# The prompt's down projection in seven Strassen products of halves, its second residual prepared during the up projection

## The chip, the cores and the metric

The kernel runs on one core of a Trainium2 chip. The time of a run is the device time in microseconds, from start to end of the program on that core. A core has a matrix engine (TensorE, PE in the profile; its weight loads are PEld), VectorE (DVE), ScalarE (ACT), GpSimd (POOL) and SyncE (SP), which issues most transfers. Each has its own queue of instructions, worked off in order; they wait for each other through semaphores.

## The reference

One layer for a prompt of 1024 tokens and a sample of 32, all in float32. The change touches only what follows the attention: the convolutional feed-forward block, and the second residual and norm.

```python
def _post_norm(x, h, gate, g, b):
    y = DEEPNORM_ALPHA * x.astype(jnp.float32) + gate.astype(jnp.float32) * h.astype(jnp.float32)
    mu = jnp.mean(y, axis=-1, keepdims=True)
    var = jnp.mean(jnp.square(y - mu), axis=-1, keepdims=True)
    return ((y - mu) * lax.rsqrt(var + LN_EPS) * g + b).astype(x.dtype)

def _conv_ffn(u, conv_prev, w_up, conv_w, conv_b, w_down):
    ...
    h = jax.nn.silu(conv) * b
    return jnp.einsum('btf,fd->btd', h, w_down), a_pad[:, -(CONV_WIDTH - 1):]

    # in _layer
    x = _post_norm(x, h, g1, ln1_g, ln1_b)
    u2 = x * (1.0 + sc2) + sh2
    f_out, conv_state = _conv_ffn(u2, conv_prev, w_up, conv_w, conv_b, w_down)
    x = _post_norm(x, f_out, g2, ln2_g, ln2_b)
```

The width of the model is 1024, that of the feed-forward block 2816, so `w_down` is 2816x1024 and the prompt's h is 1024x2816.

## The kernel before

Every large product is formed from float32 operands that are split in two (`split`, L85: ScalarE casts the value to a rounded high part, VectorE subtracts it to get the low part), and three products of the parts are summed in PSUM (`mm3`, L89). A product works on 128 rows of the contraction, 128 tokens as weights of the array and up to 512 output columns.

The stages around the change, in program order:

- The output projection (L855 and on) leaves each token block's normed result, without gain and bias, in the DRAM tile `dx1`, and its modulated transpose as `u2h` and `u2l` in SBUF.
- The up projection (L1071 to L1111) runs 22 passes `j` of 128 feed-forward columns, with two halves `s` (gate branch and the other). The weights of a half come through `up_weights` (L987) and `weights` (L860): a load on SP's queue into `raw`, the split into `wh` and `wl`, two buffers of each in the pool `pw`. After half 0 ScalarE copies the result into `row`, GpSimd sets the two columns ahead of it and keeps the convolution's state (L1087 to L1094), VectorE forms the convolution (L1095 to L1097), ScalarE applies SiLU (L1098). After half 1 VectorE multiplies into `hT[j]` (L1103 to L1105), 128 columns of h by 1056 tokens, which stays in SBUF.
- The down projection (L1115 to L1204) is `token_products` (L871): the eight blocks of 128 prompt tokens and the block of 32 sample tokens run in three groups, `groups = [[0, 1, 2, 8], [3, 4, 5], [6, 7]]`, each over 22 steps `k` of the contraction. In a step, `prepare` (L880) loads and splits a 128x1024 slice of the weights and splits a 128x384 (or 256) slice of h; it runs two steps ahead of the products, and its buffers alternate between the pools `pw` and `pf`, so that there are four of each. A step has 6 products for each prompt block (two halves of 512 columns) and 4 for the sample. In the last group the products of the last 4 steps are held and done block by block (L940).
- After a group `evacuate2` (L1143) multiplies the accumulators by the gate `g2p` out of PSUM (VectorE, L961 or L965), and later, spread over the next group's steps, adds the residual (L1148), forms the moments (L971, L975, L977 on VectorE, a power on GpSimd, L978) and scales (L1157, L1158), then stores. For the last two blocks `finish` (L1161) does this right away in small pieces.
- The second residual is ALPHA·(`dx1`·ln1_g + ln1_b). `residual` (L1134) loads a block of `dx1` and forms it on GpSimd during the down projection, 8 operations of 256 columns for a block; `begin2` (L1123) calls it late in each group.

The order of the instructions on each engine is made by the framework's scheduler from the program's order and its own estimate of times, except where `manual_schedule` stands. A tile's buffer is free for the next tile of its tag when all readers of the old one are done; a pool that is opened where another was closed waits for the old tiles at the same place.

## Time and profile before

| | us |
|---|---|
| median of 3 runs | 1597.68 |
| lowest, highest run | 1596.52, 1601.83 |
| the profiled execution, its own time | 1596.38 |
| its span in the trace | 1594.1 |

The trace is of one execution, and every number below is of that one; between its own time and its span lie 2.3 us. In a row, PE's busy time counts matmuls that overlap in the array, so a busy PE isn't yet PE at its best pace. Two records of one engine that follow each other overlap a little. A wait or a gap is put down to what ended it.

### The profile page before, as it was taken

How to read it: one execution, taken by the hardware profiler on the slowest of the kernel's cores; microseconds unless marked ns; L12 is line 12 of the kernel's file. 1: busy time of each engine (PE TensorE's matmuls, PEld its weight loads, DVE VectorE, ACT ScalarE, POOL GpSimd, SP SyncE). 2: the span in 40 equal slices, each digit the busy share in tenths (PEclk: the TensorE clock that was granted, in tenths of full speed). 3: DMA queues.
4: the chain of work that ended last, by engine and by line, in shares of the span. 5: the costliest groups of instructions: out<-in, count | busy, mean ns of one | idle time of the engine just before them, and what ended most of it. 6: DMA issues, size and time to landing. Idle time of an engine off the chain costs nothing.

```text
span 1594.1 us, 22475 instructions
## 1 busy us (share of the span) xinstructions
PE 1513.3 (95%) x8657; PEld 1266.8 (79%) x8657; DVE 798.5 (50%) x1552; ACT 569.0 (36%) x1123; POOL 365.5 (23%) x496
## 2 busy tenths in 40 slices
PE   6999999988999999899899999999999999997985
PEld 4677778755646777777799999999999988876874
DVE  4522325733536899557852333233323345377495
ACT  3211211244637788545532121112111233332342
POOL 0002014744413343134300000000000005054052
PEclk9999999998999999999999999999999999999998
DMA  9523312579764433445411111111111135344362
GB/s 270 164 95 111 94 46 107 147 194 240 196 185 119 126 77 96 125 162 207 140 54 41 53 40 53 41 53 40 54 41 54 40 129 205 106 149 135 132 207 83
DMA packets 166796, 183.83 MB, mean 115 GB/s; under 512 B 7458, under 2 KB 131907, under 8 KB 166691
## 3 DMA queue, kind: packets, MB, share of 16 engines
q1 hardware_dynamic: 158642, 155.84, 32.3%
q0 software_dynamic: 7760, 26.04, 5.6%
q8 instruction: 68, 1.11, 0.3%
q10 hardware_dynamic: 288, 0.52, 0.1%
q14 instruction: 38, 0.30, 0.1%
HBM read 151.94 MB, written 22.05 MB: 109 GB/s over the span
## 4 chain that ended last, share of the span: by engine, by line
PE 80%; DVE 7%; DMA 4%; issue 2%; POOL 2%; SPq 2%; ACT 2%; POOLq 0%; DVEq 0%; ACTq 0%
PE up L80 21%; PE upc L80 10%; PE wd L80 6%; PE wo L80 4%; PE po L80 3%; PE Sf L80 2%; PE ptf L114 2%; PE Sd L80 2%; PE pod L80 1%; POOL rs L1140 1%; SPq L171 1%; PE wd2y L80 1%; PE wd2x L80 1%; DMA wrfq<-in_w_in 1%; DMA adan<-in_w_ada 1%
## 5 line engine op out<-in xcount | busy, mean ns | idle before, releaser
L1093 POOL COPY cvo<-row 128x2 f32<-128x2 f32 x22 | 20.2, 918 | 385.4 <-ACT row L1091 385.4
L86 ACT CAST wdt<-h 128x384 fp32r<-128x384 f32 (+1 forms) x66 | 31.5, 478 | 160.4 <-PE wd5y L80 70.6
L1140 POOL TENSOR_TENSOR rs<-rs,ag 128x256 f32<-128x256 f32 x32 | 40.1, 1279 | 148.3 <-DMA rs<-dx 125.5
L625 POOL TENSOR_SCALAR wf<-wf,rs 128x128 f32<-128x128 f32 (+7 forms) x64 | 47.4, 745 | 109.2 <-DVE rs L591 71.9
L87 DVE TENSOR_TENSOR wdt<-h,wdt 128x384 fp32r<-128x384 f32 (+1 forms) x66 | 36.7, 556 | 67.8 <-ACT wdt L86 67.7
L1090 ACT COPY row<-up 128x352 f32<-128x352 f32 x44 | 17.8, 458 | 135.3 <-PE up L80 135.3
L1098 ACT ACTIVATE cv<-cv 128x1058 f32<-128x1058 f32 x22 | 24.0, 1089 | 95.5 <-DVE cv L1097 95.5
L590 ACT ACTIVATE wf<-wf,lo 128x128 f32<-128x128 f32 (+7 forms) x64 | 49.5, 776 | 18.3 <-DVE lo L587 16.0
L86 ACT CAST wh<-wr 128x512 fp32r<-128x512 f32 x40 | 24.3, 621 | 85.2 <-DMA wr<-in_w_in 19.3
L590 ACT ACTIVATE wd<-wd,lo 128x128 f32<-128x128 f32 (+7 forms) x64 | 49.6, 776 | 13.9 <-DVE lo L587 11.9
L80 PE MATMUL po<-ptpf,vf 128*64 128x256 f32 (+1 forms) x320 | 53.9, 374 | 0.5 <-DVE ptpf L615 0.4
L87 DVE TENSOR_TENSOR wh<-wr,wh 128x512 fp32r<-128x512 f32 x40 | 28.6, 738 | 51.1 <-ACT wh L86 51.1
L587 DVE CUSTOM_DVE_ANT_0 wf<-Sf,nb 128x512 f32<-128x512 f32 (+3 forms) x64 | 36.9, 589 | 28.5 <-PE Sf L80 21.3
L114 PE MATMUL ptf<-cst,wf 128*128 128x128 f32 x288 | 47.8, 287 | 1.1 <-POOL wf L625 0.7
L114 PEld LDWEIGHTS ptf<-cst,wf 128*128 128x128 f32 x288 | 32.2, 144 | 18.6 <-issue 9.3
L1103 DVE TENSOR_TENSOR h<-up,cv 128x352 f32<-128x352 f32 x44 | 21.0, 520 | 45.1 <-PE up L80 44.0
L80 PEld LDWEIGHTS po<-ptpf,vf 128*64 128x64 f32 x320 | 29.0, 138 | 18.0 <-issue 6.7
L650 POOL TENSOR_SCALAR wd<-wd,rs,lam 128x128 f32<-128x128 f32 (+7 forms) x32 | 26.5, 827 | 64.4 <-DVE rs L591 63.4
L1104 DVE TENSOR_TENSOR h<-upc,cv 128x320 f32<-128x320 f32 x22 | 10.8, 492 | 57.5 <-PE upc L80 57.5
L587 DVE CUSTOM_DVE_ANT_0 wd<-Sd,zero 128x512 f32<-128x512 f32 (+3 forms) x64 | 36.6, 583 | 1.7 <-PE Sd L80 1.3
L80 PE MATMUL pod<-ptpd,vd 128*128 128x256 f32 (+1 forms) x160 | 35.2, 362 | 0.4 <-ACT sq L667 0.3
L80 PEld LDWEIGHTS pod<-ptpd,vd 128*128 128x128 f32 x160 | 29.2, 191 | 4.4 <-ACT sq L667 0.9
(2698 smaller groups left out, 5032.9 us busy)
## 6 DMA issues: line engine op xcount, KB each, us to landing
wr<-in_w_in SPq DMA_DIRECT2D x20, 512.0 KB
adam<-in_w_ada SPq DMA_DIRECT2D x32, 256.0 KB
adan<-in_w_ada SPq DMA_DIRECT2D x32, 256.0 KB
ga<-in_w_ada SPq DMA_DIRECT2D x16, 512.0 KB
out<-z POOLq DMA_DIRECT2D x12, 512.0 KB, 4.0
x<-in_x_prompt SPq DMA_DIRECT2D x8, 512.0 KB
nb<-dcump SPq DMA_DIRECT2D x8, 512.0 KB
xp<-in_x_prompt SPq DMA_DIRECT2D x8, 512.0 KB
```

What stands on the lines that cost most here:

```text
L80: nc.tensor.matmul(out, l, r, start=start, stop=stop, **k)
L86: nc.scalar.copy(hi, src)
L87: (eng or nc.vector).tensor_tensor(lo, src, f(hi), ALU.subtract)
L114: nc.tensor.transpose(out, in_, ident[:n, :n])
L587: nc.vector.tensor_tensor_reduce(w[:, c], S[:, 0:n], t, -1.0, lo, ALU.add, ALU.min, lo_)
L590: nc.scalar.activation(w[:, 0:ext], w[:, 0:ext], AF.Exp, bias=lo, scale=-1.0, accum_out=sm)
L625: nc.gpsimd.tensor_scalar(w, w, rs, 1.0, ALU.mult, ALU.mult)
L650: nc.gpsimd.tensor_scalar(e1, e1, r1, lam, ALU.mult, ALU.mult)
L1093: nc.gpsimd.tensor_copy(cvo[:, 0, :, j], row[:, T:T + 2])
L1098: nc.scalar.activation(c[:, 0:L], c[:, 0:L], AF.Silu)
L1103: nc.vector.tensor_tensor(h[:, cs], accs[g], c[:, cs], ALU.mult)
L1140: nc.gpsimd.tensor_tensor(r[:, c], r[:, c], ag[0:n, c], ALU.mult)
```

## The change

The prompt's down projection is a product of 1024x2816 by 2816x1024. Both are cut into 2x2 halves (512 tokens; 1408 rows of the contraction, 11 steps of 128; 512 output columns), and the seven products of Strassen's scheme are formed in seven phases (`PHASES`), each with four blocks of 128 tokens by 512 columns over 11 steps, in four of six PSUM banks. Where a factor is a sum or difference, VectorE forms that of h and GpSimd that of the weights before the split. After a phase each accumulator is copied (ScalarE) or added (VectorE) into one or two quarters of the result, which is kept in SBUF as `ys`. The sample's 32 tokens are formed as before, over the weight halves that four of the phases have split anyway (`sam`). The gate is applied to the sums by GpSimd (`gate_and_add`), for blocks 0 to 3 in phase 5 and for blocks 4 to 7 in phase 6; `finish` adds the last product of blocks 4 to 7. The products of the last three steps of phase 6 are held and done block by block.

The second residual is formed during the up projection: `residuals` takes four steps in each of the first 18 passes, each a 128x128 piece of `dx1` loaded, multiplied and added on GpSimd, and stored to the new DRAM tile `dres`, from which the down projection loads blocks as they are.

The pool `pw` is closed before the down projection, and `px` is opened in its place. The operands' buffers are `xt` (two), `x2` (three, for the second slice of the weights) and `ot` (two in `px`, two in `pf`).

In the up projection:

```diff
+        def residuals():
+            for c0 in range(0, D, P):
+                c = slice(c0, c0 + P)
+                gb = pe.tile([P, 2, P], F32, name=f"gb{c0}", tag="gb", bufs=1)
+                for i, n in enumerate(("ln1_g", "ln1_b")):
+                    nc.sync.dma_start(gb[:, i], a[n][:, c].to_broadcast([P, P]))
+                nc.gpsimd.tensor_scalar(gb, gb, ALPHA, 0.0, ALU.mult, ALU.add)
+                for b in range(9):
+                    n = rows(b)
+                    r = pe.tile([P, P], F32, name=f"rr{c0}{b}", tag="rr", bufs=2)[0:n]
+                    nc.sync.dma_start(r, dx1[b * P:b * P + n, c])
+                    nc.gpsimd.tensor_tensor(r, r, gb[0:n, 0], ALU.mult)
+                    nc.gpsimd.tensor_tensor(r, r, gb[0:n, 1], ALU.add)
+                    nc.sync.dma_start(dres[b * P:b * P + n, c], r)
+                    yield
+        resid = residuals()
         for j in range(NJ):
+            for _ in range(4):
+                next(resid, None)
```

The down projection's `begin2`, `residual`, `evacuate2`, its `finish` and the call of `token_products` go, and in their place stands:

```diff
+    pwp.__exit__(None, None, None)
+    psum("psd", m=6, po=1, ms=1)
+    NK = NJ // 2
+    PHASES = [
+        (((0, 0), (1, 1), 1), ((0, 0), (1, 1), 1), ((0, 0, 1), (1, 1, 1)), None),
+        (((1, 1), None, 0), ((1, 0), (0, 0), -1), ((0, 0, 1), (1, 0, 1)), (0, "b")),
+        (((0, 0), (1, 0), 1), ((1, 1), None, 0), ((0, 0, -1), (0, 1, 1)), (1, "ab")),
+        (((0, 0), None, 0), ((0, 1), (1, 1), -1), ((0, 1, 1), (1, 1, 1)), (1, "a")),
+        (((1, 0), (1, 1), -1), ((1, 0), (1, 1), 1), ((0, 0, 1),), None),
+        (((0, 1), (1, 1), 1), ((0, 0), None, 0), ((1, 0, 1), (1, 1, -1)), (0, "ab")),
+        (((0, 1), (0, 0), -1), ((0, 0), (0, 1), 1), ((1, 1, 1),), None),
+    ]
+    HELD = 3
+    with pool("px") as px, pool("pf") as pf:
...
+        def prepare(n):
...
+            xt = px.tile([P, 2, 512], F32, name=f"xt{i}{k}", tag="xt", bufs=2)
+            ot = px.tile([P, 2, 2, 512], F32R, name=f"ot{i}{k}", tag="ot", bufs=2) if n % 4 < 2 else pf.tile([P, 2, 2, 512], F32R, name=f"ot{i}{k}", tag="ot", bufs=2)
+            w = lambda r: w_dn[:, r[0] * NK + k, r[1] * 512:(r[1] + 1) * 512]
+            h = lambda l: hT[l[0] * NK + k][:, l[1] * 512:(l[1] + 1) * 512]
+            nc.sync.dma_start(xt[:, 1], w(r0))
+            if r1:
+                x2 = px.tile([P, 512], F32, name=f"x2{i}{k}", tag="x2", bufs=3)
+                nc.sync.dma_start(x2, w(r1))
+                nc.gpsimd.tensor_tensor(xt[:, 1], xt[:, 1], x2, sign[rs_])
+            if l1:
+                nc.vector.tensor_tensor(xt[:, 0], h(l0), h(l1), sign[ls])
+                split(ot[:, 0], ot[:, 1], xt)
+            else:
+                split(ot[:, 0, 0], ot[:, 1, 0], h(l0))
+                split(ot[:, 0, 1], ot[:, 1, 1], xt[:, 1])
+            if sam:
+                x = {"a": hT[k][:, T:TT], "b": hT[NK + k][:, T:TT]}.get(sam[1])
+                if x is None:
+                    x = pt_(f"sa{i}{k}", "sa", 2, (P, TS))
+                    nc.vector.tensor_tensor(x, hT[k][:, T:TT], hT[NK + k][:, T:TT], ALU.add)
+                t = sp[n % 3]
+                split(t[:, 0:TS], t[:, TS:2 * TS], x)
+            ready[n] = ot
...
+        def gate_and_add(b, hs=range(2), eng=None):
+            for h in hs:
+                for c0 in range(h * 512, h * 512 + 512, 256):
+                    c = slice(c0, c0 + 256)
+                    nc.gpsimd.tensor_tensor(ys[b][:, c], ys[b][:, c], g2p[:, c], ALU.mult)
+                    nc.gpsimd.tensor_tensor(ys[b][:, c], ys[b][:, c], res[b][:, c], ALU.add)
...
+        def before_last(b):
+            load_residual(b)
+            gate_and_add(b)
+            half[b] = cp.tile([P, 2, 6], F32, name="st4", tag="st4", bufs=4)
+            nc.vector.bn_stats(half[b][:, 0], ys[b][:, 0:512])
+        def finish(b, acc):
+            y, st, mv = ys[b], half[b], small("mv", 2, 3)
+            c = slice(512, 1024)
+            t = pt_(f"tf{b}", "tf", 2, (P, 512))
+            nc.vector.tensor_tensor(t, acc, g2p[:, c], ALU.mult)
+            nc.vector.tensor_tensor(y[:, c], y[:, c], t, ALU.add)
+            nc.vector.bn_stats(st[:, 1], y[:, c])
+            mu, rstd = spread(st, mv, P)
...
+            d = 768
+            for c in (slice(0, d // 2), slice(d // 2, d)):
+                nc.vector.scalar_tensor_tensor(y[:, c], y[:, c], mu, lng[:, c], ALU.subtract, ALU.mult)
+                nc.vector.scalar_tensor_tensor(y[:, c], y[:, c], rstd, lnb[:, c], ALU.mult, ALU.add)
+                nc.sync.dma_start(y_p[0, b * P:(b + 1) * P, c], y[:, c])
...
+        for i, (_, _, targets, sam) in enumerate(PHASES):
+            acc = [b1(f"wd{i}{b}", "m") for b in range(4)]
...
+            for k in range(NK):
+                n = i * NK + k
+                prepare(n + 2)
+                if last and k >= NK - HELD:
+                    held.append(k)
+                else:
+                    for b in range(4):
+                        prod(b, k)
...
+                while rest and NK * (left - len(rest)) < left * (k + 1):
+                    rest.pop(0)()
...
+            for b in range(4):
+                for t, d, sg in targets:
+                    y = ys[4 * t + b][:, d * 512:(d + 1) * 512]
+                    if (t, d) not in fresh:
+                        nc.scalar.copy(y, acc[b]) if sg > 0 else nc.scalar.mul(y, acc[b], -1.0)
+                    else:
+                        nc.vector.tensor_tensor(y, y, acc[b], sign[sg])
+            fresh |= {(t, d) for t, d, _ in targets}
+            if i == 4:
+                for b in range(4):
+                    rest += [lambda b=b: load_residual(b), lambda b=b: gate_and_add(b), lambda b=b: norm(b),
+                             lambda b=b: scale(ys[b], y_p[0, b * P:(b + 1) * P], P, *st_[b])]
+            if i == 5:
+                rest += [sample_end] + [lambda b=b: before_last(b) for b in range(4, 8)]
```

## Rows read from the trace of the kernel before

**Rows 1.** The page: busy time of each engine.

```profile
PE 1513.3 (95%) x8657; PEld 1266.8 (79%) x8657; DVE 798.5 (50%) x1552; ACT 569.0 (36%) x1123; POOL 365.5 (23%) x496
```

**Rows 2.** Stretches: length, busy PE, PEld, DVE, ACT, POOL; granted clock, DMA share, GB/s.

```profile
787.00:1290.00 503.00, 500.87 (x3152) 499.27 (x3151) 177.19 (x233) 110.61 (x180) 30.11 (x92) 1.00 0.17 49
1297.70:1405.00 107.30, 106.19 (x470) 87.45 (x468) 49.65 (x72) 39.12 (x71) 23.89 (x24) 1.00 0.47 164
1405.00:1511.70 106.70, 98.08 (x420) 78.90 (x419) 71.13 (x89) 33.19 (x47) 36.89 (x36) 0.97 0.41 141
1511.70:1578.00 66.30, 61.61 (x266) 49.06 (x264) 58.97 (x82) 27.77 (x41) 22.83 (x23) 1.00 0.49 167
1578.00:1594.10 16.10, 0.00 (x0) 0.00 (x0) 6.48 (x12) 0.60 (x1) 6.80 (x9) 0.66 0.18 65
```

**Rows 3.** TensorE's waits from 1297 on: total us, times, longest.

```profile
PE wd L80 <- DVE wdw18l L87: 8.6, 1, 8.6
PE wd6x L80 <- DVE wdw25l L87: 1.8, 1, 1.8
```

**Rows 4.** Chain of waits, then TensorE's timeline: start, us, engine, line.

```profile
1459.01 2.72 PE wd L80 x12
...
1297.73 0.47 PE L80 MATMUL wd<-wdw00h,wdt 128*128 128x512 f32 x1
...
1577.37 0.39 PE L80 MATMUL wd7y<-wdw221h,wdt 128*128 128x512 f32 x1
```

**Rows 5.** Groups by shape: out<-in, count | busy us, mean ns | idle before.

```profile
L1168 DVE TENSOR_TENSOR yo<-yo,rs 128x512 f32<-128x512 f32 x4 | 2.8, 692 | 0.1
L87 DVE TENSOR_TENSOR wdw220l<-wdw220r,wdw220h 128x1024 fp32r<-128x1024 f32 x1 | 1.2, 1227 | 0.5 <-ACT wdw220h L86 0.5
L1105 DVE TENSOR_TENSOR h<-upc,cv 128x32 f32<-128x32 f32 x21 | 3.8, 181 | 0.0
L86 ACT CAST wdw012h<-wdw012r 128x1024 fp32r<-128x1024 f32 x1 | 1.1, 1056 | 0.2 <-PE wd8y L80 0.2
L1140 POOL TENSOR_TENSOR g2s<-g2s,ag 32x256 f32<-32x256 f32 x4 | 2.8, 728 | 0.0
L87 POOL TENSOR_TENSOR wow03l<-wow03r,wow03h 128x1024 fp32r<-128x1024 f32 x1 | 2.4, 2399 | 3.1 <-ACT wow03h L86 3.1
```

**Rows 6.** Timeline of GpSimd and of VectorE in the second group.

```profile
1418.89 13.56 POOL L1140 TENSOR_TENSOR rs<-rs,ag 128x256 f32<-128x256 f32 x4
1443.19 2.79 POOL L1141 TENSOR_TENSOR rs<-rs,ab 128x256 f32<-128x256 f32 x4
...
1423.02 1.39 DVE L1157 SCALAR_TENSOR_TENSOR yo<-yo,mv,lng 128x512 f32<-128x512 f32 x2
1424.81 1.21 DVE L87 TENSOR_TENSOR wdw15l<-wdw15r,wdw15h 128x1024 fp32r<-128x1024 f32 x1
1425.94 0.54 DVE L87 TENSOR_TENSOR wdt<-h,wdt 128x384 fp32r<-128x384 f32 x1
1442.74 8.81 DVE L1158 SCALAR_TENSOR_TENSOR yo<-yo,rstd,lnb 128x512 f32<-128x512 f32 x4 [11.58 <-POOL rstd L978]
```

**Rows 7.** The stretch in which TensorE restarts after the 8.6 us wait.

```profile
1449.90:1456.80 6.90, 3.60 (x9) 2.87 (x10) 6.90 (x10) 0.00 (x0) 0.00 (x0) 0.51 0.68 219
```

**Rows 8.** Timeline: one weight load's issue on SP, its cast on ScalarE.

```profile
1531.56 0.33 SPq L865 DMA_DIRECT2D wdw210r<-in_w_down  x1
...
1534.67 1.05 ACT L86 CAST wdw210h<-wdw210r 128x1024 fp32r<-128x1024 f32 x1 [0.36 <-DMA wdw210r<-in_w_down]
```

**Rows 9.** Timeline: VectorE's last operation.

```profile
1584.51 0.62 DVE L1177 SCALAR_TENSOR_TENSOR yo<-yo,rstd,lnb 128x384 f32<-128x384 f32 x1
```

**Rows 10.** Up projection: a load's issue, its cast; GpSimd's first small operation.

```profile
1265.74 0.34 SPq L865 DMA_DIRECT2D wdw00r<-in_w_down  x1
...
1286.30 1.05 ACT L86 CAST wdw00h<-wdw00r 128x1024 fp32r<-128x1024 f32 x1 [2.79 <-PE upc L80]
...
L1087 POOL MEMSET row<- 128x2 f32 x22 | 2.2, 100 | 72.7 <-DVE cv L1097 72.7
```

More of the change, by code (lines that the diff above doesn't have):

```diff
@@ L140, in layer_kernel @@
     dx1 = dp.tile([TT, D], F32, name="dx1")
+    dres = dp.tile([TT, D], F32, name="dres")
     cap = pool("ca")
@@ new lines, in layer_kernel @@
+        sign = {1: ALU.add, -1: ALU.subtract}
+        sp = [pf.tile([P, P], F32R, name=f"wds{i}", tag=f"sp{i}", bufs=1) for i in range(3)]
+        for t in sp:
+            nc.gpsimd.memset(f(t[:, 2 * TS:P]), 0.0)
+        g2p, lng, lnb = [pt_(n, n, 1) for n in ("g2p", "lng", "lnb")]
+        ys = [pt_(f"yo{b}", f"y{b}", 1) for b in range(NB)]
+        res, fresh, ready, rest = {}, set(), {}, []
+        def prepare(n):
+            if n >= len(PHASES) * NK:
+                return
+            i, k = divmod(n, NK)
+            (l0, l1, ls), (r0, r1, rs_), _, sam = PHASES[i]
+            xt = px.tile([P, 2, 512], F32, name=f"xt{i}{k}", tag="xt", bufs=2)
[21 more added lines that the diff above has]
+            ready[n] = ot
@@ new lines, in layer_kernel, with norm, scale, sample_end @@
+        st_ = {}
+        def norm(b):
+            st_[b] = moments(ys[b], P)
+        def scale(y, dst, n, mu, rstd):
+            for h in range(2):
+                c = slice(h * 512, (h + 1) * 512)
+                nc.vector.scalar_tensor_tensor(y[:, c], y[:, c], mu, lng[0:n, c], ALU.subtract, ALU.mult)
+                nc.vector.scalar_tensor_tensor(y[:, c], y[:, c], rstd, lnb[0:n, c], ALU.mult, ALU.add)
+                nc.sync.dma_start(dst[:, c], y[:, c])
+        def sample_end():
+            y, gs = pt_("ys", "rs", 3), pt_("g2s", "rs", 3)[0:TS]
+            nc.sync.dma_start(gs, dgate[1][1:2].to_broadcast([TS, D]))
+            for h in range(2):
+                nc.scalar.copy(y[:, h * 512:(h + 1) * 512], sacc[h])
+            for h in range(2):
+                c = slice(h * 512, (h + 1) * 512)
+                ps = b1("psum8", ("po", "ms")[h])
+                mm(ps[0:TS], cst[:, C_SUM:C_SUM + TS], y[:, c], True, True)
+                nc.vector.tensor_tensor(y[0:TS, c], ps[0:TS], gs[:, c], ALU.mult)
+            load_residual(8)
+            y = y[0:TS]
+            nc.vector.tensor_tensor(y, y, res[8][0:TS], ALU.add)
+            scale(y, y_s[0], TS, *moments(y, TS))
@@ L1205, in layer_kernel @@
     hp_.__exit__(None, None, None)
-    pwp.__exit__(None, None, None)
     banks["cm"].__exit__(None, None, None)
```

115 lines of the change are left out of this document (39 added, 76 removed).

## The prediction

> **What bounds the kernel now.** I read the page first for TensorE's share of the span [rows 1], then the table of stretches [rows 2]. The change touches two of them: the up projection, where TensorE is busy 500.87 of 503 us, and the down projection, three stretches with 106.19 of 107.3, 98.08 of 106.7 and 61.61 of 66.3 us, and then the tail of 16.1 us, with no product in it. So the end is set by the products, and the question is whether fewer of them still set it. The list of TensorE's waits [rows 3] says what breaks the stretch today: one wait of 8.6 us and two of 1.8 us, all ended by VectorE. From the chain of waits and the timeline [rows 4] I take the pace, 12 products in 2.72 us (0.2267 us each), the first product at 1297.73 and the end of the last at 1577.76. That is 280.0 us for 8·2·22·3 + 22·4 = 1144 products, which alone need 1144/12·2.72 = 259.3 us; 20.7 us are waits and restarts.
>
> **The products.** Seven phases of 11 steps of 4 blocks of 3 products are 924, and four phases carry 2 products of the sample in each step, 88: together 1012, or 229.4 us. The saving is 29.9 us, and up to 20.7 us more if no wait remained. One step takes 12 products, 2.72 us, in phases 0, 4 and 6 and 14 products, 3.17 us, in phases 1, 2, 3 and 5; the phases 29.9 and 34.9 us.
>
> **What a step must be fed with.** In the kernel before a step needs one cast and one subtraction of the weights and one of the tokens. After, it also needs sums: VectorE adds two slices of h (128x512) in phases 0, 2, 4, 5, 6, and GpSimd adds two slices of weights (128x512) in phases 0, 1, 3, 4, 6. Durations [rows 5]: a VectorE sum of 512 columns 0.69 us, the subtraction of 1024 columns 1.23, a small one 0.18, ScalarE's cast of 1024 columns 1.06. GpSimd takes 0.73 us for 256 columns and 2.40 for 1024; 512 lie at 0.73 + 256·(2.40 − 0.73)/768 = 1.28 (estimate). Back to back, records overlap: four GpSimd sums in 2.79 us are 0.70 each, and VectorE's next starts 0.08 to 0.1 us before the end of a record [rows 6].
>
> These two engines don't run beside each other here. While VectorE worked without a break (17 operations, three rows of which stand there), four GpSimd sums, 2.8 us of work, took 13.56 us; while GpSimd then had a row of sums, four VectorE operations, two of which take 1.39 us, took 8.81 us [rows 6]. Both read two operands from SBUF. So I add them up. The Trainium skill, page "SBUF — State Buffer", section "Who interferes with whom", states it more sharply: a VectorE instruction with two SBUF inputs and a GpSimd instruction that reads SBUF exclude each other, and whichever began holds the ports for its whole instruction. The trace agrees in kind (13.56 us for 2.8 us of work). By the whole records a step of phase 0 would be 0.69 + 1.23 + 1.28 = 3.20 us in place of the 2.98 below, phases 5 and 6 together 124 us in place of 114, and the total some 10 us above mine.
>
> **Phases 0 and 4** (h sum, weight sum, subtraction of 1024): back to back 0.61 + 1.13 + 1.24 = 2.98 us of VectorE and GpSimd a step, over the 2.72 of the products. There is a second limit: `xt` has two buffers where the kernel before has four raw ones. A buffer is loaded, added into by GpSimd, cast, subtracted from, and only then loaded again. Load to cast takes 3.1 us for 512 KB [rows 8], which I keep for the two loads of 256 KB; 3.1 + 1.28 + 1.06 + 1.23 = 6.7 us, half of it 3.34 us a step. Each phase 37 us; low 33 (the 2.98), high 43 (each turn of the loop waits for one VectorE operation of the other buffer, +0.6 us a step).
>
> **Phases 1 and 3** (weight sum, two subtractions of 512): loop 3.1 + 1.28 + 0.62 + 0.69 = 5.7, half 2.85; ports 1.24 + 1.22 + 0.15 = 2.6; products 3.17. 35.5 us each (34.9 to 38). **Phase 2** (h sum alone): loop (3.1 + 1.06 + 1.23)/2 = 2.7; products bound, 34.9 us (to 36).
>
> **Phases 5 and 6** also carry the end of the layer. In phase 5 blocks 0 to 3 are gated, normed and scaled, in phase 6 the sample is finished and blocks 4 to 7 are gated. A block's gating is 8 GpSimd sums, 5.6 us; its scaling 4 VectorE operations of 0.66. Phase 5 holds the ports 11·(0.61 + 1.13 + 0.15 + 0.15) = 22.4, plus 4·5.6 = 22.4, plus 16·0.66 = 10.6: 55 us against 34.9 of products. Phase 6: 11·2.98 = 32.8, plus 22.4, plus 3.8 for the sample (a sum of 1024 columns and four scalings): 59 against 29.9. VectorE's and GpSimd's queues are in order, so the next step's sums stand behind this work, and `ot` holds only two steps ahead of TensorE. I take the sum of the ports, 114 us; low 97 (15% less, as every record of 0.7 us has some 0.05 us at each end that overlapped its neighbour), high 130 (whole records, 124, and the handing over). The residual products that the old stage did on GpSimd (64 sums of 0.7 us) leave this stage, but the gating, which VectorE did on the way out of PSUM, takes their place with 64.
>
> **The rest.** Start: `px` has exactly the 30 KB of `pw`, so the first `ot` lies where the last up weights lie; its cast (1.06) and subtraction (1.23) can't begin before the last up product. Before, the first weights were cast at 1286.30, 11 us early [rows 10]. +2 us (0.5 to 4). Ends of phases: four accumulators of six are wanted again, evacuated by ScalarE or VectorE in 0.6 to 0.7 us each while TensorE has two free ones: +2 (0 to 5). Tail: `finish` is 0.69·3 + 0.21 + 0.15 + 4·0.62 = 4.9 us of VectorE for each of four blocks, 19.6, beginning 27 products (6.1 us) before the last one, so VectorE ends 13.5 us after it; before it ended 7.4 us after it [rows 4, 9]. +5 us (1 to 8).
>
> Up projection: 72 residual steps of two loads or stores on SP and two GpSimd sums of 128 columns (under 0.73 us each), four steps in each of 18 passes of 22.9 us. SP waits at each store for its load and the sums, 3.1 + 1.4 = 4.5 us, 18 us a pass, and the up weights' loads queue behind that. What hides it: weights are issued some 20 us before they are cast [rows 10]. GpSimd's small copies for `row` also queue behind the sums; 72.7 us of GpSimd's idle time in 22 passes stood before them, so they are early. I cost the up projection at 0 (0 to 4); without the cover a pass would grow by up to 5 us, 90 in all.
>
> **Sum.** Down: 2 + 2·37 + 2·35.5 + 34.9 + 114 + 2 = 297.9 against 280.0, +17.9; tail +5; up 0: +22.9 us. Made against the profiled execution (1596.38 us, its span 1594.1): 1619.3. That execution is 1.3 us under the median of the runs, so 1620.
>
> **The rivals.**
> 1. *The products stay the bound.* The sums slip in beside TensorE. For it: phases 1 to 3 have room, and in the last stretch before VectorE was busy 58.97 of 66.3 us and GpSimd 22.83, at a loss of only 4.7 us [rows 2]. Against: phases 5 and 6. With the low ends, 0.5 + 2·29.9 + 3·34.9 + 97 = 262, that is −18, tail +2: 1581 us. If nothing at all waited, 231.4 us and the tail +5, it would be 1554.
> 2. *The two cancel:* low ends in phases 0 to 4 and in the tail, the middle in 5 and 6: 1 + 66 + 104.7 + 105 + 2 = 279: 1593 to 1602.
> 3. *One engine starves the other* (slower still). A burst of 8 gating sums keeps VectorE out, as in [rows 6], TensorE runs dry and restarts at a granted clock of 0.51 of full speed, the 1.2 GHz level, at which 9 products took 3.60 us in place of 2.0 [rows 7]. The one such stall of before cost 8.6 + 1.6 us; eight of them are 82 us over the 64.8 us of products, 33 more than the 49 that I have: 1653. It decides once the steps in stock (two) are shorter than a burst, 5.4 against 5.6 us.
> 4. *The residual steps hold up the up projection* through SP: from some 10 us of delay per load on; 1640 to 1700.
>
> **How the numbers follow.** Forecast (1604 to 1652) 0.52; rival 1 0.22; rival 2 0.12; rival 3 0.10; rival 4 0.04. A measurement of this kernel tells about 0.3%, 5 us, from no change. Faster is rival 1, 0.22; the same is rival 2, 0.12; slower the rest, 0.66. The range for 8 in 10 goes from 1583 (the low ends of all terms come to 1587, and below it part of rival 1) to 1652 (the high ends of the ports and of the loop together). The forecast's own range is 1604 to 1652.
>
> **What would show it.** Right: TensorE's waits in phases 0 and 4 are ended by ScalarE's cast or VectorE's subtraction of `ot` at 3.0 to 3.6 us a step, phases 2 and 3 run at 3.17, phases 5 and 6 take 100 to 125 us, with GpSimd's gating records far over 0.73 us or VectorE's over 0.74. Wrong: 12 products in 2.72 us through phases 0, 4 and 6; or phases 5 and 6 in under 90 us; or waits of the up products. If GpSimd's and VectorE's records keep their short durations side by side, the adding up was the mistake.

## The result and the profile after

The changed kernel takes 1681.65 us (median of 4 runs, 1674.07 to 1683.96) against 1597.10 for the kernel before (4 runs, 1594.45 to 1601.83): a ratio of 1.0518, interval 1.0476 to 1.0559. The sign was forecast, the size was not: 1620 was predicted, the range ended at 1652. The profiled execution took 1681.73 us, its span is 1679.9.

The table of stretches, cut at the first and last up product and at the first product of a phase (counted off in TensorE's timeline, 132 products in phases 0, 4 and 6, 154 in the others). Columns as in [rows 2]; the stretches are the up projection, phase 0, phases 1 to 3, phase 4, phases 5 and 6, and the tail.

```profile
785.90:1338.80 552.90, 525.17 (x3198) 519.18 (x3196) 179.87 (x232) 109.19 (x178) 112.83 (x244) 0.97 0.21 61
1344.90:1392.20 47.30, 37.00 (x133) 26.97 (x134) 24.11 (x24) 13.89 (x17) 14.81 (x11) 0.88 0.55 195
1392.20:1500.50 108.30, 106.21 (x463) 86.12 (x462) 66.17 (x116) 47.62 (x98) 30.37 (x23) 1.00 0.40 136
1500.50:1543.10 42.60, 34.37 (x134) 25.00 (x133) 28.65 (x36) 11.26 (x13) 25.33 (x23) 0.96 0.37 125
1543.10:1657.90 114.80, 81.81 (x291) 59.29 (x289) 93.59 (x127) 24.11 (x32) 75.05 (x70) 0.85 0.33 113
1657.90:1679.90 22.00, 0.00 (x0) 0.00 (x0) 12.16 (x24) 1.80 (x3) 8.78 (x12) 0.55 0.20 73
```

Read it against [rows 2]. The up projection, which TensorE filled before, is 552.9 us long for the same products that took 510.4 before (first product at 787.43, end of the last at 1297.86, where the first down product starts [rows 4]): 42.5 us, half of the loss. Then 6.1 us pass without a product of the down projection (1338.8 to 1344.9), its seven phases take 313.0 us against 280.0, and the tail 22.0 against 16.3. Together 87 us; the up projection began 1.5 us earlier, and the spans differ by 85.8.

The waits of TensorE's products say who ended the gaps, first over the whole up projection, then from 1340 us on (total us, times, longest):

```profile
PE up L80 <- ACT wu51h L86: 5.8, 1, 5.8
PE up L80 <- ACT wu71h L86: 4.0, 1, 4.0
PE up L80 <- ACT wu61h L86: 3.6, 1, 3.6
PE up L80 <- ACT wu91h L86: 3.4, 1, 3.4
PE up L80 <- ACT wu81h L86: 3.1, 1, 3.1
...
PE wd L80 <- ACT ot L86: 34.9, 16, 9.0
PE wd L80 <- DVE ot L87: 21.1, 12, 7.3
```

The first five lines are new: each of passes 5 to 9 stood for the cast of its second weight, and the cast for its load, the first of them so:

```profile
ACT wu51h L86 <- DMA wu51r<-in_w_up: 10.7, 1, 10.7
```

These five waits are 19.9 us, all gaps between up products that are longer than 0.3 us come to 25.6 us more than before, and the other 17 us of the 42.5 are products at a lower clock behind the gaps: after the first gap 17 products take 5.37 of 6.8 us, at a granted clock of 0.51 (1.2 GHz), as in [rows 7].

```profile
926.00:932.80 6.80, 5.37 (x17) 4.92 (x18) 1.22 (x1) 1.04 (x1) 2.86 (x7) 0.51 0.15 43
```

### The profile page after: what moved, and what is told of

It reads as the page before. It is cut to its first block, busy times and chain, and to the rows that moved or that the text cites. A ratio compares the mean times of both kernels' runs of the same rounds, so it can differ in the third digit from the quotient of the medians.

```text
span 1679.9 us, 22888 instructions
## 1 busy us (share of the span) xinstructions
PE 1527.9 (91%) x8525; PEld 1263.9 (75%) x8525; DVE 839.4 (50%) x1630; ACT 567.5 (34%) x1128; POOL 513.5 (31%) x697
## 4 chain that ended last, share of the span: by engine, by line
PE 53%; DMA 17%; DVE 13%; POOL 8%; issue 4%; ACT 3%; SPq 2%; POOLq 0%; ACTq 0%; DVEq 0%
PE up L80 12%; PE upc L80 6%; DVE ot L87 4%; DMA rr<-dx 4%; DMA xt<-in_w_down 4%; PE wo L80 3%; DMA dres<-rr 3%; PE po L80 3%; POOL rr L1089 2%; PE Sf L80 2%; PE ptf L114 2%; ACT ot L86 2%; POOL rr L1090 2%; PE Sd L80 2%; POOL xt L1180 2%
## 5 line engine op out<-in xcount | busy, mean ns | idle before, releaser
L80 PE MATMUL wd<-ot 128*128 128x512 f32 x924 | 245.9, 414 | 56.5 <-ACT ot L86 34.9
L80 PEld LDWEIGHTS wd<-ot 128*128 128x128 f32 x924 | 180.5, 200 | 114.0 <-ACT ot L86 42.5
L87 DVE TENSOR_TENSOR ot<-xt,ot 128x1024 fp32r<-128x1024 f32 (+1 forms) x77 | 93.4, 1214 | 90.9 <-ACT ot L86 90.2
L86 ACT CAST ot<-xt 128x1024 fp32r<-128x1024 f32 (+1 forms) x77 | 71.4, 928 | 196.6 <-POOL xt L1180 149.9
L1180 POOL TENSOR_TENSOR xt<-xt,x 128x512 f32<-128x512 f32 x55 | 72.1, 1319 | 156.8 <-DMA xt<-in_w_down 59.6
L1115 POOL COPY cvo<-row 128x2 f32<-128x2 f32 x22 | 13.6, 616 | 231.0 <-ACT row L1113 231.0
L1089 POOL TENSOR_TENSOR rr<-rr,gb 128x128 f32<-128x128 f32 (+1 forms) x72 | 44.6, 627 | 111.0 <-DMA rr<-dx 110.2
L86 ACT CAST wh<-wr 128x512 fp32r<-128x512 f32 x40 | 24.3, 621 | 85.8 <-DMA wr<-in_w_in 20.1
L114 PEld LDWEIGHTS ptf<-cst,wf 128*128 128x128 f32 x288 | 33.5, 148 | 19.4 <-issue 10.2
L1090 POOL TENSOR_TENSOR rr<-rr,gb 128x128 f32<-128x128 f32 (+1 forms) x72 | 41.4, 587 | 2.4
```

The lines of the kernel that those rows point to most:

```text
L80: nc.tensor.matmul(out, l, r, start=start, stop=stop, **k)
L86: nc.scalar.copy(hi, src)
L87: (eng or nc.vector).tensor_tensor(lo, src, f(hi), ALU.subtract)
L114: nc.tensor.transpose(out, in_, ident[:n, :n])
L1089: nc.gpsimd.tensor_tensor(r, r, gb[0:n, 0], ALU.mult)
L1090: nc.gpsimd.tensor_tensor(r, r, gb[0:n, 1], ALU.add)
```

## Experiments

Lengths in us, from each kernel's timeline cut in the same way; "start" is from the last up to the first down product. e3 and all kernels built on it (e4 to e11 and e15) leave the first norm's gain and bias out of the residual. Medians are compared with the kernel before on the same chip. How early the up projection begins differs between kernels by up to 16 us (778.6 to 794.9), though nothing ahead of it was edited, so the stretches are the finer comparison.

| kernel | up | start | phases 0 / 1 / 2 / 3 / 4 | 5 and 6 | tail | median | ratio |
|---|---|---|---|---|---|---|---|
| predicted | 510 | 2 | 37 / 35.5 / 34.9 / 35.5 / 37 | 114 | 21 | 1620 | |
| after | 552.9 | 6.1 | 47.3 / 38.1 / 35.4 / 34.9 / 42.5 | 114.8 | 22.0 | 1681.65 | 1.0518 |
| e1 | 517.0 | 6.1 | 47.0 / 38.7 / 36.8 / 34.9 / 41.5 | 113.2 | 18.4 | 1639.46 | 1.0264 |
| e2 | 548.7 | | the down projection of before | | | 1637.51 | 1.0241 |
| e14 | 523.0 | 6.4 | 46.3 / 38.3 / 37.0 / 34.9 / 43.0 | 113.8 | 23.2 | 1653.11 | one run |
| e16 | 510.5 | 6.1 | 46.5 / 38.3 / 36.7 / 34.9 / 41.8 | 114.3 | 22.4 | 1637.37 | 1.0295 |
| e3 | 510.6 | 6.0 | 46.3 / 37.4 / 37.0 / 34.9 / 41.7 | 113.3 | 23.0 | 1632.43 | 1.0214 |
| e4 | 510.8 | 2.4 | 45.3 / 38.1 / 35.9 / 34.9 / 29.9 | 99.1 | 21.8 | 1603.82 | 1.0045 |
| e5 | 510.5 | 6.2 | 41.4 / 37.0 / 36.8 / 34.9 / 42.2 | 118.2 | 21.0 | 1634.76 | 1.0233 |
| e6 | 510.5 | 5.9 | 47.0 / 37.7 / 36.7 / 34.9 / 37.3 | 96.7 | 22.0 | 1616.70 | 1.0136 |
| e7 | 510.6 | 6.1 | 46.3 / 38.1 / 36.5 / 34.9 / 39.7 | 110.8 | 22.2 | 1631.41 | 1.0220 |
| e8 | 510.4 | 6.1 | 37.3 / 35.3 / 34.9 / 34.9 / 36.0 | 112.0 | 22.1 | 1614.25 | 1.0118 |
| e9 | 510.8 | 6.0 | 37.6 / 35.2 / 34.9 / 34.9 / 33.5 | 101.5 | 23.1 | 1605.89 | 1.0063 |
| e10 | 510.8 | 6.0 | 37.6 / 36.2 / 34.9 / 34.9 / 31.1 | 84.4 | 21.8 | 1583.82 | 0.9910 |
| e11 | 510.8 | 5.5 | 36.4 / 34.9 / 34.9 / 34.9 / 32.4 | 97.7 | 22.6 | 1598.80 | 1.0021 |
| e15 | 510.4 | 5.5 | 36.5 / 34.9 / 34.9 / 34.9 / 33.0 | 97.7 | 22.1 | 1596.83 | 1.0005 |
| e12 | 510.5 | 5.5 | 34.6 / 34.9 / 34.9 / 34.9 / 33.6 | 97.6 | 17.5 | 1593.72 | 0.9977 |
| e13 | 510.4 | 2.4 | 36.8 / 34.9 / 34.5 / 35.5 / 32.6, in its own order | 99.5 | 16.7 | 1592.42 | 0.9974 |

Half-widths of the ratios' intervals are 0.0013 (e15) to 0.0066 (e2); they are given where a verdict hangs on them.

### The up projection: one part alone, and the queue

```diff
 # e1_res_pool_queue: all three kinds of transfer of residuals()
-                    nc.sync.dma_start(r, dx1[b * P:b * P + n, c])
+                    nc.gpsimd.dma_start(r, dx1[b * P:b * P + n, c])
 # e2_before_plus_res: residuals() and its four calls a pass, put into the kernel before
```

> The loads (lines 1083 and 1088) and the stores (line 1091) of the 72 residual steps are issued by GpSimd and no longer by SP; nothing else changes. Theory Q (the up projection lost its 42 us because its weight loads stand in SP's program behind residual loads and stores that wait for GpSimd): its stretch falls from 552.9 us to about 510 to 518, the matmuls wait for no cast of wu any more, and the run takes about 1640 (1632 to 1650). Rival P (GpSimd's own 144 sums, and their lock against VectorE, hold up the row copies on ScalarE): the stretch stays at 545 to 560 and the run at 1675 to 1690; if GpSimd now stands still at its own loads, the waits of ScalarE's row copies for cvo grow.

> The kernel before with the residual steps of the change added to its up projection (what they store is read by nobody; the down projection is the old one). If the two parts of the change are separate (theories Q and P alike), it loses the up projection's 42 us and nothing else: 1635 to 1645. Rival: the stretching comes from how the new down projection's instructions are queued with the up projection; then it stays within 5 us of 1597.

e2 says that the two parts are separate: the residual steps alone stretch the old kernel's up projection to 548.7 us and cost 40 us (1637.51 against 1597.66). e1 says where: the same sums, the same transfers, issued by another engine, and 36 of the 42 us are gone. Rival P keeps the remaining 6.4 us: in e1 ScalarE's row copies waited 104.6 us for GpSimd's small copies `cvo`, since GpSimd now stands at its own loads.

What SP did in the changed kernel stands in its own list of waits, from 780 to 1060 us, and in its timeline between two loads of weights:

```profile
SPq L1091 <- POOL rr L1090: 103.5, 45, 5.1
SPq L1088 <- DMA dres<-rr: 46.5, 42, 2.9
```

```profile
903.61 0.43 SPq L866 DMA_DIRECT2D wu50r<-in_w_up  x1
905.17 0.32 SPq L1091 DMA_DIRECT2D dres<-rr  x1
...
913.02 1.76 SPq L1091 DMA_DIRECT2D dres<-rr  x2
914.88 1.47 SPq L1088 DMA_DIRECT2D rr<-dx  x2
918.91 2.20 SPq L1091 DMA_DIRECT2D dres<-rr  x2
921.78 0.32 SPq L1088 DMA_DIRECT2D rr<-dx  x1
922.19 0.38 SPq L866 DMA_DIRECT2D wu51r<-in_w_up  x1
```

SP waits at most of the 72 stores for the sums (line 1091, 45 waits) and at most of the 72 loads until a buffer's last store has landed (line 1088, 42 waits). Between two weight loads lie five stores, that is five residual steps, 18.6 us here and 15.6 to 17.1 in the passes before it. A pass needs two weights in 22.9 us. Ten steps a pass, not four: the steps are used up by 1053 us, in the first half of the projection, and from wu100r on the loads run ahead again and there is no gap. Two readings are left: any wait of SP ahead of a weight costs, or the number of steps does. Two runs told them apart.

```diff
 # e14_rr6_sp
-                    r = pe.tile([P, P], F32, name=f"rr{c0}{b}", tag="rr", bufs=2)[0:n]
+                    r = pe.tile([P, P], F32, name=f"rr{c0}{b}", tag="rr", bufs=6)[0:n]
 # e16_four_a_pass: the steps of pass j can't start before pass j-1 has made its h
+                    nc.gpsimd.tensor_copy(r[0:1, 0:1], hT[now[-1] - 1][0:1, 0:1])
                     nc.sync.dma_start(r, dx1[b * P:b * P + n, c])
```

> The changed kernel with six buffers in place of two for the residual rows, all on SP as it is. If SP stands at the loads, which wait until a buffer's last store has landed, the up projection falls from 552.9 to 515 to 530 us. If it stands at the stores, which wait for GpSimd's sums, it stays at 545 to 556, and weights loads still stand behind stores.

> The changed kernel, where each residual step's buffer first takes a copy of one element (GpSimd) of the h tile that the pass before finished, so that no more than four steps can run in a pass, over 18 passes; loads and stores stay on SP. If the number of steps per pass was the mistake: four steps take SP 13 to 16 us of a pass's 22.9, the weights stay ahead, the up projection takes 510 to 516 us and the run 1634 to 1646. If any waiting store on SP's queue delays the weights: 18 passes grow by 1 to 3 us each, up projection 530 to 565, run over 1655.

e14: 523.0 us; with loads that run ahead a step takes SP 1.8 us (nine between two weights, 15 to 17 us), and one gap of 3.9 us and some under 1 us are left. e16: 510.5 us and 1637.37, with loads and stores on SP as in the change, and SP waits more than in the changed kernel (the lines below, 780 to 1300 us; its line 1089 is the load, which here also waits for the step's turn, 1092 the store). So it is not that SP waits at all: four steps a pass fit in front of the weights, ten don't.

```profile
SPq L1089 <- POOL rr L1088: 107.9, 39, 6.0
SPq L1092 <- POOL rr L1091: 100.1, 40, 4.4
```

### Strassen alone, and what feeds its steps

```diff
 # e3_strassen_alone: no residuals(); the rows themselves are loaded
-            nc.sync.dma_start(res[b][0:n], dres[b * P:b * P + n])
+            nc.sync.dma_start(res[b][0:n], dx1[b * P:b * P + n])
 # e4_no_wsum: e3, and
-                nc.gpsimd.tensor_tensor(xt[:, 1], xt[:, 1], x2, sign[rs_])
 # e5_late_loads: e3, and g2p, lng, lnb are loaded from step 22 on, residual rows 0 to 2 after phase 4
+                nc.scalar.copy(t[0:1, 0:1], ys[0][0:1, 0:1])
 # e8_xt3: e3, and
-            xt = px.tile([P, 2, 512], F32, name=f"xt{i}{k}", tag="xt", bufs=2)
+            xt = (px if n % 3 < 2 else pf).tile([P, 2, 512], F32, name=f"xt{i}{k}", tag="xt", bufs=2 if n % 3 < 2 else 1)
```

> The changed kernel without the residual steps in the up projection: the down projection loads the normed rows themselves, so the gain and bias of the first norm are left out of the residual. Everything else of Strassen's form stays. If the parts are separate: up projection back to about 510, first product of the down projection some 3 us after it, down projection and tail 335 to 341 us, run 1632 to 1642. Rival (the residual's late stores hold up the first loads of the down projection, so that phase 0's 47.3 us are its doing): phase 0 about 37 us and the run 1622 to 1632.

> As e3_strassen_alone, and the 44 sums of weight halves on GpSimd are left out (the second half is still loaded, but only the first is split and multiplied). Theory X (in phases 0, 4 and 6 the step waits for load, sum on GpSimd and split, with two xt buffers, and GpSimd's sums lock VectorE out): phases 0, 4 and 6 fall towards the products' 35 us, phase 5+6 to 95 to 105 because the gating stays, the run to 1605 to 1618. Rival R (the splits on ScalarE and VectorE and the transfers set these phases): phases 0 and 4 stay above 40 and the run within 8 us of e3_strassen_alone.

> As e3_strassen_alone (no residual steps, rows of the first norm without gain and bias as residual), but the six loads of 512 KB that nobody needs before phase 5 (g2p, lng, lnb, and the first three residual rows) are made to wait, by a copy of one element that ScalarE takes from the accumulated blocks, until phase 1 has ended (the three) and until phase 4 has ended (the rows). Theory L (3 MB ahead of the step loads make phase 0 long): its 46.3 us fall to 36 to 39, its steps to 3.2 to 3.5 us from the first on, run 1620 to 1626. Rival (phase 0 is long by its empty start and by the clock, not by these loads): 44 to 47 us, run 1629 to 1636. If the rows then come too late for the gating, phase 5 grows by up to 3 us.

> As e3_strassen_alone, with three buffers for xt in place of two. Loop theory (load, sum, cast and subtraction of one buffer, 6.7 us, over two buffers set phases 0, 1 and 4): with three 2.2 us a step, so that phases 0, 1 and 4 fall by 4, 2 and 5 us or more, and the run to 1615 to 1622. Port theory (VectorE and GpSimd exclude each other, 2.98 us a step and the gating): phases 0, 1, 4 within 2 us of e3_strassen_alone and the run 1626 to 1636.

e3: without the residual steps Strassen's form still loses 35 us, and phase 0 is nearly as long as in the changed kernel (46.3 against 47.3), so the residual stores are not its cause; its start is 6.0 us, not the 3 expected. e4: without the weight sums phase 4 runs at the products' pace, 134 products' records in 30.00 us without a break, and phases 5 and 6 lose 14 us; the run comes just under its range. Phase 0 barely moves (45.3), but it is no clean test there: the second halves, which nobody reads, were loaded as fast as they could be (298 GB/s over its 45.3 us, against 199 in e3).

```profile
1462.30:1492.30 30.00, 30.00 (x134) 24.73 (x133) 25.59 (x31) 9.97 (x11) 12.25 (x13) 1.00 0.24 81
```

e8 gave the most: one more buffer for `xt`, and phases 0, 1, 2 and 4 fall by 9.0, 2.1, 2.1 and 5.7 us, the ratio from 1.0214 to 1.0118 (some 15 us). The loop theory's figures, 4, 2 and 5 or more, hold, and the run is just under its 1615; the port theory (VectorE's and GpSimd's times add up and set these phases, which then stay within 2 us) falls for them. e5 is half a hit: phase 0 lost 4.9 us, not 7 to 10, and the run nothing. The three rows are now loaded together at 1495.0, as phase 5 begins, GpSimd's gating waits 6.0 us for one of them, and phases 5 and 6 grew by some 5; that the rows are the cause of all of that isn't shown.

What phase 0 of the changed kernel starts with stands in its SP timeline. Three loads of 512 KB stand in among the first steps' halves, and three rows of as much follow:

```profile
1295.67 0.57 SPq L1176 DMA_DIRECT2D xt<-in_w_down  x1
1339.21 0.33 SPq L1133 DMA_DIRECT2D out<-cvr  x1
1339.65 0.34 SPq L1179 DMA_DIRECT2D x<-in_w_down  x1
...
1341.22 0.93 SPq L1179 DMA_DIRECT2D x<-in_w_down  x2
1342.19 0.43 SPq L1268 DMA_DIRECT2D g2p<-dgate  x1
1342.67 0.43 SPq L1268 DMA_DIRECT2D lng<-in_ln_g  x1
1343.14 0.43 SPq L1268 DMA_DIRECT2D lnb<-in_ln_b  x1
```

In the first 5 us of the phase the transfers run at 331 GB/s, and 13 products take 5.00 us, at a granted clock of 0.56 (the row under this). The weights' half for the third step, issued at 1347.66, lets GpSimd's sum start only at 1356.39, and TensorE stands 6.0 us for the cast behind it:

```profile
1345.00:1350.00 5.00, 5.00 (x13) 3.94 (x14) 4.37 (x4) 1.05 (x1) 2.06 (x1) 0.56 0.89 331
```

```profile
1356.39 1.26 POOL L1180 TENSOR_TENSOR xt<-xt,x 128x512 f32<-128x512 f32 x1 [9.18 <-DMA xt<-in_w_down]
...
1358.78 7.85 PE L80 MATMUL wd<-ot 128*128 128x512 f32 x24 [6.03 <-ACT ot L86]
```

The SP lines above also hold the 6.1 us of the start. The first half of the first weights was loaded at 1295.67, the second only at 1339.65, after the end of the last up product (1338.78). Ahead of it in SP's program stands a store of the convolution's state (`cvr`, line 1133), which is complete only after the last up pass; SP stood at it for 42.9 us:

```profile
SPq L1133 <- ACT cvr L1132: 42.9, 1, 42.9
```

Whether the second half's buffer, which lies in the place of the up weights' pool, was free any earlier isn't shown. GpSimd's sum follows at 1342.48, the cast at 1343.77 and the first product at 1344.87:

```profile
1342.48 1.26 POOL L1180 TENSOR_TENSOR xt<-xt,x 128x512 f32<-128x512 f32 x1 [14.31 <-DMA x<-in_w_down]
...
1343.77 1.04 ACT L86 CAST ot<-xt 128x1024 fp32r<-128x1024 f32 x1 [3.52 <-POOL xt L1180]
...
1344.87 1.65 PE L80 MATMUL wd<-ot 128*128 128x512 f32 x3 [5.27 <-ACT ot L86]
```

e4 and e13, whose first step has no sum and so needs no second half, start after 2.4 us.

### Phases 5 and 6

```diff
 # e6_no_gating: e3 without the two lines; e10: the same on e8
-                    nc.gpsimd.tensor_tensor(ys[b][:, c], ys[b][:, c], g2p[:, c], ALU.mult)
-                    nc.gpsimd.tensor_tensor(ys[b][:, c], ys[b][:, c], res[b][:, c], ALU.add)
 # e7_gate_vector: e3 with them on VectorE, 512 columns each; e9: the same on e8
 # e11_xt3_wsum_vector: e8, and
-                nc.gpsimd.tensor_tensor(xt[:, 1], xt[:, 1], x2, sign[rs_])
+                nc.vector.tensor_tensor(xt[:, 1], xt[:, 1], x2, sign[rs_])
 # e15_no_lock: e8, gating and weight sums both on VectorE
```

> As e3_strassen_alone, and the 64 gating sums on GpSimd (gate and residual of all prompt blocks) are left out. Theory G (gating, weight sums, h sums, scalings share the ports and add up in phases 4 to 6): phases 4 to 6 lose about the 45 us that the gating holds the ports for: from 155 us to 108 to 120, phase 4 about 33 to 37; run 1585 to 1600. Rival (the xt loop of load, sum, cast, subtraction alone makes them long; the gating fits in the gaps): 145 to 155 us, run 1620 to 1633.

> As e3_strassen_alone, with the gating on VectorE, 4 operations of 512 columns a block (32 of 0.69 us, 22 us) in place of 64 of GpSimd (45 us). Theory G: 23 us less on the ports in phases 4 to 6: from 155 us to 128 to 138, run 1607 to 1617. Rival (the engines work side by side, and what counts is VectorE's own time): VectorE has 22 us more to do, phases 4 to 6 grow to 160 to 177 us and the run to 1637 to 1655.

> e8_xt3 with the gating on VectorE (32 operations of 512 columns in place of GpSimd's 64 of 256); the residual's gain and bias are left out as there. In e8_xt3 phases 5 and 6 still take 112 us. Port theory (VectorE's and GpSimd's time adds up): 23 us less, phases 5 and 6 86 to 95 us, run 1588 to 1598. Queue theory (the weight sums stand behind runs of up to 16 gating sums in GpSimd's program): the weight sums are now free of them, phases 5 and 6 80 to 95 us too, but the waits that stay are for VectorE's subtractions. Rival V (VectorE's program is what is late, whoever does the gating): 108 to 125 us, run 1610 to 1625.

> e8_xt3 without the gating (gate and residual of the prompt's blocks left out). With two buffers that was worth 16 us of the run. Port theory: 45 us less, phases 5 and 6 67 to 75 us, run 1568 to 1580. Queue theory: about the same, 66 to 75. Rival V: phases 5 and 6 stay above 85 us, because norms, scalings and the sample's end still stand in VectorE's program, run 1585 to 1600.

> e8_xt3 with the weight sums on VectorE in place of GpSimd; the gating stays on GpSimd, the residual's gain and bias are left out. Port theory: a weight sum holds the ports for 0.69 us in place of 1.26, so phases 5 and 6 lose 5 to 7 us (105 to 108) and the run 5 to 10. Queue theory (the sums wait behind gating in GpSimd's program): phases 5 and 6 fall to 80 to 95 us and the run to 1585 to 1600.

> e8_xt3 with both the weight sums and the gating on VectorE (operations of 512 columns); GpSimd keeps only the small operations of the norms; the residual's gain and bias are left out. If VectorE's and GpSimd's mutual exclusion sets phases 5 and 6, what falls out is the difference of durations: 45 us of GpSimd gating become 22 of VectorE, from e11_xt3_wsum_vector's 97.7 to 80 to 90 us, run 1583 to 1592. If the exclusion costs little and VectorE's program is the bound, its 22 us more show: 105 to 120 us, run 1606 to 1622.

The port theory is my own from the prediction, and its figures fail. (Its rivals: the queue theory, that weight sums stand behind gating in GpSimd's program, and rival V, that VectorE's program is late whoever does the gating.) Phases 4 to 6 take 134.0 us in e6 (expected 108 to 120) and 150.5 in e7 (128 to 138; the run within 1 us of e3). With three buffers, phases 5 and 6 take 101.5 in e9 (86 to 95), 84.4 in e10 (67 to 75; rival V said above 85 and 1585 to 1600, the run came to 1583.82), 97.7 in e11, between the two theories' figures, and 97.7 in e15, between the 80 to 90 and 105 to 120 expected there. The stretch of phases 5 and 6 in e8, e10 and e15 (columns as above):

```profile
1476.60:1588.60 112.00, 78.79 (x291) 56.76 (x289) 95.55 (x124) 23.11 (x31) 78.50 (x70) 0.89 0.34 112
```

```profile
1480.50:1564.90 84.40, 74.57 (x289) 56.90 (x287) 80.15 (x121) 22.19 (x29) 26.72 (x19) 0.90 0.41 134
```

```profile
1483.20:1580.90 97.70, 79.76 (x291) 59.45 (x289) 95.66 (x160) 23.65 (x31) 16.96 (x9) 0.86 0.39 128
```

In e15 GpSimd has 9 records left, mostly on single columns, and VectorE is busy 95.66 of 97.70 us: its own program is the bound. In its groups the gating is 16.2 us of that (25 records) and the weight sums 7.4; 72 us are left that are VectorE's in every one of these kernels. My sum had 56 for it. What it lacked stands in the groups of the same stretch, the adding up out of PSUM and the statistics:

```profile
L1309 DVE TENSOR_TENSOR yo<-yo,wd 128x512 f32<-128x512 f32 x12 | 7.7, 681 | 0.0
...
L972 DVE BATCH_NORM_STATS2 st<-yo 128x6 f32<-128x512 f32 x7 | 4.4, 679 | 0.0
L1238 DVE BATCH_NORM_STATS2 st<-yo 128x6 f32<-128x512 f32 x4 | 2.7, 674 | 0.0
```

With 72 us of VectorE's own, adding up comes out better for two kernels. GpSimd's 11 weight sums at 1.26 are 14 us (1.26 by the record at 1342.48 above); of the 64 gating sums 50 lie in these phases (the groups of e8 count 24 and 26), 35 us at the 0.70 of [rows 6]. That makes 72 + 14 = 86 for e10 (84.4 measured) and 72 + 16 + 14 = 102 for e9 (101.5), within 2 us both. So these lengths fit VectorE's time and GpSimd's weight sums adding up; the 72 and the 16 are from e15, and no run with three buffers leaves out the weight sums and the gating together, which would show it. With gating on GpSimd the sum is too high: 72 + 14 + 35 = 121 for e8 (112.0) and 72 + 7 + 35 = 114 for e11 (97.7). Part of it hides: some VectorE operations aren't held up by GpSimd. In e11 six adds out of PSUM take 3.67 us, 0.61 each, no longer than in e15, where GpSimd does no sums beside them (12 in 7.7 us, 0.64 each, the first row above), while GpSimd runs seven gating sums in 5.32, 0.76 each, against 0.73 for one in [rows 5].

```profile
1523.96 3.67 DVE L1310 TENSOR_TENSOR yo<-yo,wd 128x512 f32<-128x512 f32 x6
1524.72 5.32 POOL L1202 TENSOR_TENSOR yo<-yo,g2p 128x256 f32<-128x256 f32 x7 [3.96 <-DVE yo L1310]
```

The Trainium skill, page "SBUF — State Buffer", section "Who interferes with whom", says that a VectorE instruction with at most one input from SBUF doesn't contend with GpSimd, outside the two-port performance modes. These six read their other operand from PSUM, and the trace agrees (0.61 and 0.76 us).

The other half of the answer is the order in GpSimd's program, the queue theory. In the changed kernel twelve gating sums stand in a row before the next weight sum; the cast behind it waits 13.49 us, the two weight steps in stock don't last that long, and TensorE's longest wait for a cast in the list of the first section, 9.0 us, is the one that follows:

```profile
1598.39 13.35 POOL L1205 TENSOR_TENSOR yo<-yo,g2p 128x256 f32<-128x256 f32 x12
...
1611.70 1.26 POOL L1180 TENSOR_TENSOR xt<-xt,x 128x512 f32<-128x512 f32 x1
...
1612.99 1.04 ACT L86 CAST ot<-xt 128x1024 fp32r<-128x1024 f32 x1 [13.49 <-POOL xt L1180]
```

Taking the weight sums out of that row (e11) gave 14.3 us in these phases, where the shorter operation alone would have given 5 to 7. By the sums above 17 us of the gating are hidden now, in e8 it was 9. With e9 and e15 the row is gone too, but the gating has become VectorE's, and so neither is shorter in these phases than e11. How much of the 112 us is the two engines' keeping each other out and how much the order, these runs don't part further.

### The causes together

```diff
 # e12_all_repairs: the changed kernel with e1's queue and six buffers, e8's third xt buffer, e11's sums, and
+                q, late = divmod(n - 2 * NK, 3)
+                if not late and 0 <= q < 6:
+                    first = f(ready[n][0:1, 0, 0, 0:1])
...
+                        nc.scalar.copy(t[0:1, 0:1], first)
+                        nc.sync.dma_start(t, src.to_broadcast([P, D]))
 # e13_reordered: e12 with PHASES in the order 2, 3, 0, 1, 4, 5, 6, and after the second of them
+                rest += [lambda b=b: gate_and_add(b, (1,)) for b in range(3)]
```

> The whole computation of the changed kernel, with what the runs so far pointed to: the residual steps' loads and stores on GpSimd's queue with six buffers, three xt buffers, the weight sums on VectorE, and the six loads of 512 KB issued one by one, three steps apart, from phase 2 on (each waits for a copy of one element out of that step's operand). If the causes found add up: up projection 511 to 517 us, phase 0 32 to 34, phases 1 to 3 34.9 each, phase 4 32 to 34, phases 5 and 6 about 98, start 6 and tail 22: run 1592 to 1603, no longer slower than before by over 0.5%. If something else costs as well: over 1610.

> e12_all_repairs with the seven phases in the order 2, 3, 0, 1, 4, 5, 6, so that the second half of the columns of blocks 0 to 3 is complete after two phases, and with its gating for blocks 0 to 2 spread over the next ones; the six loads start in the first phase. Nothing is left out. If VectorE's and GpSimd's load at the end is what counts, the phases that come fifth and sixth lose 5 to 12 us, and the first one, which has no weight sum, starts 1 us earlier: run 1580 to 1594, faster than before. If the early gating only starves the phases that it goes to: within 4 us of e12_all_repairs.

The repairs add up: 1593.72 us, 0.9977 of the kernel before (0.9962 to 0.9991), 88 us under the changed kernel, with the up projection at 510.5 and phase 0 at 34.6. So nothing large is missing from the list of causes. The tail fell too, to 17.5; e1, with the same queue, has 18.4, and why isn't shown. e13, 1592.42 (0.9974, 0.9960 to 0.9988), came into its range but not for its main reason: phases 5 and 6 did not get shorter (99.5), the start did (2.4 us, no sum in the first step). The two can't be told apart. Both lie 0.2 to 0.3% under the kernel before, and their intervals end just under 1: hardly more than no change. Of the 29.9 us of saved products some 3 are left: phases 5 and 6, 97.6 us for 64.8 of products, take the most.

## Why the prediction was wrong

*The up projection, 0 predicted, 42.5 measured: the step that failed.* I costed the residual "four steps in each of 18 passes", as the source asks for them, and let 18 us a pass hide behind the weights' 20 us of lead [rows 10]. Four a pass would have been hidden: e16 shows it, with 510.5 us. But what the source asks for early and nothing holds back is put into SP's program as early as its buffers allow (five steps between two weights with two buffers, nine with the six of e14), and that was ten a pass. At the 3.2 us that a step took SP (16 us for five), less than my 4.5, that is 32 us a pass against 22.9, and the lead of 20 us was used up by pass 5. This was rival 4, with its place and its mechanism right and its range (1640 to 1700) holding the result, some 20 us of the other terms included; a chance of 0.04 was too little, since I had the price per step and never asked how many could run in a pass. With this step right the forecast would have held by its number: e16, 1637.37, lies in 1604 to 1652, though the terms below were off by 20 us.

*The start, 2 predicted, 6.1 measured.* I had taken the place of `ot`, under the last up weights, as the limit and counted the cast and the subtraction behind the last up product, not the load of the second half, which stands behind a waiting store in SP's program, and the sum ahead of them. Load, sum and cast are 2.8 + 1.3 + 1.1 from 1339.65 on.

*Phase 0, 37 predicted (33 to 43), 47.3 measured.* The loop of two buffers is right: from the fifth step on a step takes 3.5 us (3.34 predicted), and with e8's third buffer 2.8 from the sixth on. What I left out is in the first four steps, 22.9 us in place of 13.4: the six loads of 512 KB that the new code issues right behind its first steps (4.9 us by e5), and products at the lower clock (0.56 in the first 5 us). The two aren't parted further. With three buffers and VectorE's sums the phase takes 36.4 (e11), with these loads spread as well 34.6 (e12).

*Phases 1 to 3: 38.1, 35.4, 34.9 against 35.5, 34.9, 35.5.* Phases 2 and 3 are right; phase 1 lies just over the top of its range (38). I had the products as their limit, but with a third buffer (e8) all three are at 34.9 to 35.3, so the two buffers still held up phase 1, and phase 2 in most runs.

*Phase 4, 37 predicted, 42.5 measured.* Half of the columns of blocks 0 to 3 is complete after phase 3, and GpSimd began to gate it here: of its 23 records in that stretch 14 are gating sums. Without gating (e6) it takes 37.3.

*Phases 5 and 6, 114 predicted, 114.8 measured: a right number from a wrong sum.* My 114 were 56 of VectorE, 45 of gating and 14 of weight sums. VectorE's own work is 72; of the gating, 35 lie in these phases, and some 9 of these hide. The errors, 16 one way, 10 and 9 the other, nearly cancelled (the 9 is from e8, with its third buffer). That the steps stand behind the gating in the queue I had said, but not that it decides how much of the gating hides: 9 us, or 17 in e11.

*Tail, 21 predicted, 22.0 measured,* and the products' pace and the phases' 29.9 and 34.9 us: right.

The down projection's terms miss by 21 us (start 4, phase 0 10, phase 4 5.5, phase 1 2.6, the rest under 1 or with the other sign), the up projection by 42.5: together the 62 us between 1620 and 1681.65, within some 2 us. Rival 1, that the products stay the bound, didn't come near even in e12, where phases 1 to 3 do run at the products' pace.

## What to carry to other kernels

Work that is put "beside" a busy stretch is spread over it only if something makes it wait its turn; otherwise it bunches at the start of the stretch, and one must ask how many of its steps fit on the queue between two transfers that the bound engine needs, and which waiting store stands ahead of the next one. Where fewer products are bought with sums, the bound moves to the engines that prepare them: count every instruction of these engines in that stretch, evacuations and statistics too, and the buffers of the loop from load to release. A sum that lands on the measured number proves none of its terms; take one term away and see.
